# A decoder layer on one core: in the last feed-forward half, one weight group in four gets its low parts from an adding transfer

## The chip, the cores and the metric

The kernel runs on one core of one Trainium2 chip. The metric is the time of one execution on the device in microseconds (us); lower is better. A core has five engines that run side by side and wait for one another by semaphores: TensorE (PE, with its weight loads as PEld), VectorE (DVE), ScalarE (ACT), GpSimd (POOL) and SyncE (SP), which here only issues transfers. Transfers are moved by 16 DMA engines that SP's queue (q1) and POOL's queue (q0) share.

## What is computed

One layer of a decoder on 256 tokens of width 2048, in float32: a SwiGLU half-step, a mixer with three branches (gated linear attention, spatial gating, attention into a memory), a second SwiGLU half-step, and a final norm. The change is in the second half-step:

```python
D_MODEL = 2048; SEQ = 256; D_FF = 5632

def swiglu(h, w_gate, w_up, w_down):
    return (jax.nn.silu(h @ w_gate) * (h @ w_up)) @ w_down

def reference(x, ...):
    x = x + 0.5 * swiglu(rmsnorm(x, ffn1_norm[l]), ffn1_w_gate[l], ffn1_w_up[l], ffn1_w_down[l])
    h = rmsnorm(x, mix_norm[l])
    mem_n = rmsnorm(mem, mem_norm[l])
    x = x + mixer(h, mem_n, ...)
    x = x + 0.5 * swiglu(rmsnorm(x, ffn2_norm[l]), ffn2_w_gate[l], ffn2_w_up[l], ffn2_w_down[l])
    return rmsnorm(x, final_norm)
```

## The kernel before

Every large product is made three times in a shorter float format. A float32 number is split into a high part, its value cast to that format (`fp32r` in the rows), and a low part, the number less its high part. `products` (L122) issues, for a weight tile of 128 rows by 512 columns and a block of 128 tokens, high times high (L123), high times low weight (L124) and low times high weight (L125), all into one accumulator in PSUM.

`gemm` (L127) goes over a column block of 512 weight columns in groups of four weight tiles (512 rows, 1 MB). For each group `load` (L106) issues one transfer on SP's queue into a `raw` buffer, of which there are three. Each group is then taken in two halves of two tiles: ACT casts the half to `wh` (L119), VectorE subtracts to make `wl` (L120), and TensorE makes 12 matmuls with it. `wh` and `wl` have three buffers each, so ACT can be at most three halves ahead of TensorE.

The second half-step is the call of `ffn` (L309) with `final=True`. It works in two parts of 6 and 5 column blocks. A block is a `gemm` with the gate weights (16 weight tiles, so groups at 0, 4, 8 and 12), the Silu on ACT (L319), a `gemm` with the up weights, the product on VectorE (L323), and the transposition and splitting of the result (L166 on TensorE, L174 on ACT, L175 on VectorE), which TensorE reaches during the first group of the next `gemm`. After each part come four `gemm` calls with the down weights.

Larger or longer-lived tiles take one of 17 slots (`slot`, named `m8` or `m_` with a number in the rows). In the second half-step the input, the residual, the final gain and the hidden tiles of a part hold 13 of them.

The text of the kernel doesn't set the order on an engine by itself: a scheduler orders the instructions of each engine when the program is built, with costs of its own. Each engine then runs its list strictly in that order.

Of the kernel before, what the change touches and what calls it, by code (L numbers as in the profile page):

```python
# [8 lines left out]
F32 = mybir.dt.float32  # L9
# [8 lines left out]
P = 128  # L18
# [5 lines left out]
CW = 512  # L24
# [35 lines left out]
def layer(ctx: ExitStack, tc: tile.TileContext, a: dict, out: bass.AP):  # L60
# [10 lines left out]
    def slot(shape, dtype=F32):  # L71
        return big.tile(shape, dtype, name="m8", tag="m8")
# [33 lines left out]
    def load(w, row, col, parts=1):  # L106

        raw = wp.tile([P, 4, CW], F32, name="raw", tag="raw")
        n = 4 // parts
        for i in range(0, 4, n):  # L110
            r = row + i * P
            nc.sync.dma_start(
                raw[:, i : i + n, :],
                w[r : r + n * P, col : col + CW].rearrange("(j p) n -> p j n", p=P),
            )
        return raw

    def split(raw, wh, wl):
        nc.scalar.copy(wh, raw)  # L119
        nc.vector.tensor_tensor(wl, raw, wh.bitcast(F32), op=ALU.subtract)  # L120
# [3 lines left out]
        nc.tensor.matmul(acc, lhsT=lhs.h(kt, b), rhs=wl, start=False, stop=False)  # L124
        nc.tensor.matmul(acc, lhsT=lhs.l(kt, b), rhs=wh, start=False, stop=last)  # L125

    def gemm(lhs, n_tiles, w, row0, col0, accs, ticks=0, raws=(), tail=0):  # L127


        raws = list(raws)  # L130
        held = []
        for g0 in range(0, n_tiles, 4):
            raw = raws.pop(0) if raws else load(w, row0 + g0 * P, col0)
            late = g0 >= n_tiles - 4 * tail
            if late:
                both = [slot([P, 4, CW], F32R) for _ in range(2)]
                held.append((g0, *both))
            for h0 in (0, 2):
                if late:
                    wh, wl = (t[:, h0 : h0 + 2, :] for t in both)  # L140
                else:
                    wh = wp.tile([P, 2, CW], F32R, name="wh", tag="wh")
                    wl = wp.tile([P, 2, CW], F32R, name="wl", tag="wl")
                split(raw[:, h0 : h0 + 2, :], wh, wl)
                if late:
                    continue
                for b in range(NB):
                    for j in range(2):
                        kt = g0 + h0 + j
                        products(  # L150
                            lhs, kt, b, wh[:, j, :], wl[:, j, :], accs[b],
                            kt == 0, kt == n_tiles - 1,
                        )
                tick(ticks)
        for b in range(NB):
            for g0, wh, wl in held:
                for j in range(4):
                    kt = g0 + j
                    products(
                        lhs, kt, b, wh[:, j, :], wl[:, j, :], accs[b], kt == 0, kt == n_tiles - 1  # L160
                    )
# [147 lines left out]
    def ffn(xT, rs, wg, wu, wd, after, begin=lambda: None, final=False):  # L309
        done = 0  # L310
        for part, n_ch in enumerate((6, 5)):
            hT = Split(slot, 4 * n_ch)
            for c in range(n_ch):
                col = (done + c) * CW
                pg = [acc() for _ in range(NB)]
                gemm(xT, KT, wg, 0, col, pg, ticks=1)
                sil = [tmp() for _ in range(NB)]
                for b in range(NB):
                    nc.scalar.activation(sil[b], pg[b], AF.Silu, scale=rs[:, b : b + 1])  # L319
                pu = [acc() for _ in range(NB)]  # L320
                gemm(xT, KT, wu, 0, col, pu, ticks=1)
                for b in range(NB):
                    nc.vector.scalar_tensor_tensor(  # L323
                        out=sil[b], in0=pu[b], scalar=rs[:, b : b + 1], in1=sil[b],
                        op0=ALU.mult, op1=ALU.mult,
                    )
                    tsplit(sil[b], hT, 4 * c, b)
# [493 lines left out]
```

## Time and profile before

| | |
|---|---|
| median of 2 runs | 2392.0 us (2391.84 to 2392.16) |
| the profiled execution | 2390.98 us, of which the span from the first to the last instruction is 2389.3 us |
| TensorE busy | 2371.3 us, 99% of the span |
| VectorE busy | 1269.8 us, 53% |
| ScalarE busy | 1071.5 us, 45% |
| GpSimd busy | 59.6 us, 2% |
| SP's DMA queue | 442.56 MB, 56.9% of the 16 engines' time |
| gate and up blocks of the second half-step, part one | about 1636 to 1900 us of the span |

Busy shares are means over the whole span. Which engine sets the end is read from who waits for whom, and TensorE's clock from the granted clock of a stretch (1.00 is 2.4 GHz, 0.50 is 1.2 GHz).

### The profile page before, as it was taken

The page shows a single profiled execution, that of the slowest core. Times are in us where ns is not written, and L with a number is a line of the kernel's source. Part 1 is how long each engine was busy: PE and PEld are TensorE (multiplying, and loading weights), DVE is VectorE, ACT ScalarE, POOL GpSimd, SP SyncE. Part 2 cuts the span into 40 slices and gives each one's busy share as a digit, 9 for nine tenths or more (in the row PEclk, how much of TensorE's full clock was granted, in tenths as well). Part 3 has the DMA queues.
Part 4 walks back from the last instruction along what each step waited for, and adds up shares of the span by engine and source line. Part 5 has one row for each costly group of instructions (what it writes and reads, how often), then busy time and mean ns, then how long its engine had stood idle before and what let it go on. Part 6 is the DMA issues. An engine that isn't in the chain of part 4 may idle for free.

```text
span 2389.3 us, 26431 instructions
## 1 busy us (share of the span) xinstructions
PE 2371.3 (99%) x10746; PEld 1961.4 (82%) x10746; DVE 1269.8 (53%) x1330; ACT 1071.5 (45%) x1265; POOL 59.6 (2%) x57
## 2 busy tenths in 40 slices
PE   8999999999999999999999999999999999999998
PEld 6888888888888888888788888888888888888886
DVE  5644545445445556556765555555454454454454
ACT  7544444344444444435444444445444433444443
POOL 0000000000000001001200000000000000000000
PEclk9999999999999999999999999999999999999999
DMA  7565565565566665444546556655555555555564
GB/s 263 185 191 188 186 193 194 194 193 188 184 193 196 196 207 194 147 167 159 177 159 212 194 194 194 204 184 191 186 188 192 194 189 193 192 184 193 194 191 144
DMA packets 224211, 451.76 MB, mean 189 GB/s; under 512 B 7268, under 2 KB 7336, under 8 KB 223448
## 3 DMA queue, kind: packets, MB, share of 16 engines
q1 hardware_dynamic: 222344, 442.56, 56.9%
q0 software_dynamic: 1744, 7.51, 0.9%
q8 instruction: 84, 1.38, 0.2%
q14 instruction: 39, 0.32, 0.0%
HBM read 445.84 MB, written 4.19 MB: 188 GB/s over the span
## 4 chain that ended last, share of the span: by engine, by line
PE 97%; DVE 1%; issue 1%; ACT 1%; DMA 0%; ACTq 0%; POOLq 0%; POOL 0%; SPq 0%; DVEq 0%
PE acc L124 31%; PE acc L123 31%; PE acc L125 31%; PE trp L166 2%; PE sml L641 0%; DVE wl L120 0%; PE sml L546 0%; PE sml L574 0%; PE sml L449 0%; DMA m<-in_mem_dram 0%; ACT m L658 0%; ACT tmp L180 0%; ACT wh L119 0%; PE sml L695 0%; PE sml L508 0%
## 5 line engine op out<-in xcount | busy, mean ns | idle before, releaser
L120 DVE TENSOR_TENSOR wl<-raw,wh 128x1024 fp32r<-128x1024 f32 x828 | 1029.2, 1244 | 1024.5 <-ACT wh L119 1023.9
L119 ACT CAST wh<-raw 128x1024 fp32r<-128x1024 f32 x828 | 871.4, 1053 | 1161.3 <-PE acc L125 1144.5
L124 PE MATMUL acc<-wl,m 128*128 128x512 f32 x3312 | 1294.4, 391 | 1.8 <-DVE wl L120 1.8
L125 PE MATMUL acc<-wh,m 128*128 128x512 f32 x3312 | 1290.4, 390 | 0.1
L123 PE MATMUL acc<-wh,m 128*128 128x512 f32 x3312 | 1183.7, 392 | 1.8 <-ACT wh L119 0.9
L124 PEld LDWEIGHTS acc<-wl,m 128*128 128x128 f32 x3312 | 622.5, 188 | 132.2 <-DVE wl L120 3.3
L123 PEld LDWEIGHTS acc<-wh,m 128*128 128x128 f32 x3312 | 622.0, 188 | 131.3 <-ACT m L190 2.2
L125 PEld LDWEIGHTS acc<-wh,m 128*128 128x128 f32 x3312 | 622.1, 188 | 127.5 <-DVE m L191 0.5
L190 ACT ACTIVATE m<-trp,gT 128x128 fp32r<-128x128 f32 x128 | 43.0, 364 | 23.7 <-PE trp L166 14.3
L174 ACT CAST m<-trp 128x512 fp32r<-128x512 f32 x64 | 34.9, 588 | 40.9 <-PE trp L166 40.9
L175 DVE TENSOR_TENSOR m<-trp,m 128x512 fp32r<-128x512 f32 x64 | 41.7, 686 | 21.2 <-ACT m L174 20.9
L191 DVE SCALAR_TENSOR_TENSOR m<-trp,gT,m 128x128 fp32r<-128x128 f32 x128 | 41.3, 347 | 13.5 <-ACT m L190 12.3
L166 PEld LDWEIGHTS trp<-ident,tmp 128*128 128x128 f32 x288 | 34.7, 140 | 6.6
L166 PE MATMUL trp<-ident,tmp 128*128 128x128 f32 x288 | 40.0, 272 | 0.0
L319 ACT ACTIVATE tmp<-acc,rs 128x512 f32<-128x512 f32 x44 | 30.1, 690 | 19.5 <-PE acc L125 19.5
L180 ACT ACTIVATE tmp<-m 128x512 f32<-128x512 f32 x40 | 24.8, 623 | 15.6 <-DVE m L338 11.9
L323 DVE SCALAR_TENSOR_TENSOR tmp<-acc,rs,tmp 128x512 f32<-128x512 f32 x44 | 30.9, 743 | 0.0
L338 DVE SCALAR_TENSOR_TENSOR m<-acc,m 128x512 f32<-128x512 f32 x32 | 20.9, 683 | 9.8 <-PE acc L125 9.5
L203 POOL TENSOR_TENSOR rs<-rs,mhalf 128x1 f32<-128x1 f32 x8 | 4.4, 554 | 868.7 <-DVE rs L200 868.7
L166 PE MATMUL trp<-ident,m 128*128 128x128 f32 x160 | 22.8, 280 | 2.9 <-DMA m<-in_mem_dram 2.9
L166 PEld LDWEIGHTS trp<-ident,m 128*128 128x128 f32 x160 | 19.7, 144 | 6.6 <-DMA m<-in_mem_dram 3.0
L661 POOL TENSOR_TENSOR m<-m,m 128x1024 f32<-128x1024 f32 x7 | 20.9, 2992 | 115.3 <-ACT m L658 87.8
(136 smaller groups left out, 389.0 us busy)
## 6 DMA issues: line engine op xcount, KB each, us to landing
raw<-in_w_in_dram SPq DMA_DIRECT2D x96, 1024.0 KB, 5.1
raw<-in_ffn_w_gate_dram SPq DMA_DIRECT2D x88, 1024.0 KB, 5.2
raw<-in_ffn_w_up_dram SPq DMA_DIRECT2D x88, 1024.0 KB, 5.2
raw<-in_ffn_w_down_dram SPq DMA_DIRECT2D x88, 1024.0 KB, 5.1
raw<-in_w_branch_dram SPq DMA_DIRECT2D x24, 1024.0 KB, 5.1
raw<-in_w_out_dram SPq DMA_DIRECT2D x16, 1024.0 KB, 5.1
raw<-in_w_kv_mem_dram SPq DMA_DIRECT2D x14, 1024.0 KB, 5.1
m<-in_mem_dram SPq DMA_DIRECT2D x4, 512.0 KB, 8.3
```

The costliest lines, as they stand in the source:

```text
L119: nc.scalar.copy(wh, raw)
L120: nc.vector.tensor_tensor(wl, raw, wh.bitcast(F32), op=ALU.subtract)
L123: nc.tensor.matmul(acc, lhsT=lhs.h(kt, b), rhs=wh, start=first, stop=False)
L124: nc.tensor.matmul(acc, lhsT=lhs.h(kt, b), rhs=wl, start=False, stop=False)
L125: nc.tensor.matmul(acc, lhsT=lhs.l(kt, b), rhs=wh, start=False, stop=last)
L166: nc.tensor.transpose(out=ps[:, j * P : (j + 1) * P], in_=src[:, j * P : (j + 1) * P], identity=ident)
L174: nc.scalar.copy(hi, ps)
L175: nc.vector.tensor_tensor(lo, ps, hi.bitcast(F32), op=ALU.subtract)
L190: nc.scalar.activation(dst.h(kt, b), pj, AF.Copy, scale=g)
L191: nc.vector.scalar_tensor_tensor(out=dst.l(kt, b), in0=pj, scalar=g, in1=dst.h(kt, b).bitcast(F32), op0=ALU.mult, op1=ALU.subtract,)
L319: nc.scalar.activation(sil[b], pg[b], AF.Silu, scale=rs[:, b : b + 1])
L323: nc.vector.scalar_tensor_tensor(out=sil[b], in0=pu[b], scalar=rs[:, b : b + 1], in1=sil[b], op0=ALU.mult, op1=ALU.mult,)
```

## The change

In the gate and up products of the second half-step, the group at row 12 x 128 of each column block (the last of four) is no longer split by VectorE. A new function loads the group on SP's queue as before, lets ACT cast it to the high part `wh`, lets ACT also write the negated high part into `wl`, and issues on POOL's queue a second transfer of the same megabyte of weights that adds to `wl` in place. Both tiles are of four weight tiles and take slots of the 17 instead of the three-deep `wh` and `wl` buffers. The function is called at the head of `gemm`, so its load is issued ahead of the loads of groups 0, 4 and 8. There are 22 such groups, two for each of the 11 column blocks.

```diff
+    def split_by_dma(w, row, col):
+        raw = load(w, row, col)
+        wh, wl = (slot([P, 4, CW], F32R) for _ in range(2))
+        for h0 in (0, 2):
+            hs = slice(h0, h0 + 2)
+            nc.scalar.copy(wh[:, hs, :], raw[:, hs, :])
+            nc.scalar.activation(wl[:, hs, :], wh[:, hs, :].bitcast(F32), AF.Copy, scale=-1.0)
+        nc.gpsimd.dma_start(
+            wl,
+            w[row : row + 4 * P, col : col + CW].rearrange("(j p) n -> p j n", p=P),
+            accum_op=ALU.add,
+        )
+        return wh, wl
+
-    def gemm(lhs, n_tiles, w, row0, col0, accs, ticks=0, raws=(), tail=0):
+    def gemm(lhs, n_tiles, w, row0, col0, accs, ticks=0, raws=(), tail=0, added=None):
...
+        if added is not None:
+            sums = split_by_dma(w, row0 + added * P, col0)
         for g0 in range(0, n_tiles, 4):
-            raw = raws.pop(0) if raws else load(w, row0 + g0 * P, col0)
+            if g0 == added:
+                raw = None
+            else:
+                raw = raws.pop(0) if raws else load(w, row0 + g0 * P, col0)
...
             for h0 in (0, 2):
-                if late:
+                if g0 == added:
+                    wh, wl = (t[:, h0 : h0 + 2, :] for t in sums)
+                elif late:
                     wh, wl = (t[:, h0 : h0 + 2, :] for t in both)
...
-                split(raw[:, h0 : h0 + 2, :], wh, wl)
+                if raw is not None:
+                    split(raw[:, h0 : h0 + 2, :], wh, wl)
...
-                gemm(xT, KT, wg, 0, col, pg, ticks=1)
+                gemm(xT, KT, wg, 0, col, pg, ticks=1, added=12 if final else None)
...
-                gemm(xT, KT, wu, 0, col, pu, ticks=1)
+                gemm(xT, KT, wu, 0, col, pu, ticks=1, added=12 if final else None)
```

The scheduler places the new instructions. In the changed kernel's text the lines after the new function are 24 further down (L319 becomes L343, L166 becomes L190, L174 becomes L198), the new casts are L134, the negating copies L135 and the adding transfers L136.

ACT's list in the second column block of part one, gate product: before, from the cast of the second half of group 4 on. The two L174 rows split the transposed result of the block ahead, `wh_11987` and `wh_12003` are group 8, `wh_12021` and `wh_12037` group 12, and `wh_12061` opens the up product.

```order
L119 CAST wh_11969<-raw_11951 128x1024
L174 CAST m8_11613<-trp_11900 128x4x128
L174 CAST m8_11613<-trp_11908 128x4x128
L119 CAST wh_11987<-raw_11985 128x1024
L119 CAST wh_12003<-raw_11985 128x1024
L119 CAST wh_12021<-raw_12019 128x1024
L119 CAST wh_12037<-raw_12019 128x1024
L119 CAST wh_12061<-raw_12059 128x1024
```

The same place on ACT in the changed kernel. `m8_11917` is the high part of group 12, `m8_11918` its negated copy that the adding transfer completes; `m8_12058` and `m8_12059` are the pair of the up product.

```order
L119 CAST wh_11976<-raw_11958 128x1024
L198 CAST m8_11613<-trp_11898 128x4x128
L134 CAST m8_11917<-raw_11915 128x1024 x2
L198 CAST m8_11613<-trp_11906 128x4x128
L135 ACTIVATE m8_11918<-m8_11917 128x1024
L119 CAST wh_11994<-raw_11992 128x1024
L135 ACTIVATE m8_11918<-m8_11917 128x1024
L119 CAST wh_12010<-raw_11992 128x1024
L134 CAST m8_12058<-raw_12056 128x1024 x2
L119 CAST wh_12067<-raw_12065 128x1024
L135 ACTIVATE m8_12059<-m8_12058 128x1024 x2
```

The casts and copies for this group 12 stand between group 4 and group 8 of the same product, the ones for the up product's group 12 already before its group 0 is done.

TensorE's list at the end of that gate product, before: `wh_12037` and `wl_12038` are the second half of group 12, and `acc_12057`, `acc_12058` the accumulators of the up product.

```order
L124 MATMUL acc_11916<-wl_12038,m8_10912 128x512
L125 MATMUL acc_11916<-wh_12037,m8_10914 128x512
L123 MATMUL acc_11916<-wh_12037,m8_10912 128x512
L124 MATMUL acc_11916<-wl_12038,m8_10912 128x512
L125 MATMUL acc_11916<-wh_12037,m8_10914 128x512
L123 MATMUL acc_12057<-wh_12061,m8_10911 128x512
L123 MATMUL acc_12058<-wh_12061,m8_10911 128x512
L124 MATMUL acc_12057<-wl_12062,m8_10911 128x512
```

The same engine in the changed kernel where group 8 ends and group 12 begins. The first row that reads `m8_11918` waits for POOL's transfer.

```order
L125 MATMUL acc_11914<-wh_12010,m8_10914 128x512
L123 MATMUL acc_11913<-m8_11917,m8_10912 128x512
L123 MATMUL acc_11914<-m8_11917,m8_10912 128x512
L123 MATMUL acc_12054<-wh_12067,m8_10911 128x512
L123 MATMUL acc_12055<-wh_12067,m8_10911 128x512
L124 MATMUL acc_11913<-m8_11918,m8_10912 128x512
L125 MATMUL acc_11913<-m8_11917,m8_10914 128x512
L123 MATMUL acc_11913<-m8_11917,m8_10912 128x512
L124 MATMUL acc_11913<-m8_11918,m8_10912 128x512
```

Two matmuls of the up product have moved ahead of the first use of the sum; everything behind that row waits with it.

POOL's list around the start of the second half-step, before and then in the changed kernel (`rs_3` is the scale of the norm that the first Silu needs):

```order
L756 DMA m8_10915<-kept_984 128x2048
L756 DMA m8_10916<-kept_984 128x2048
L284 DMA m8_11611<-in_final_norm_dram 128x2048
L203 TENSOR_TENSOR rs_3_10910<-rs_11601,mhalf_84 128x1
L203 TENSOR_TENSOR rs_3_10910<-rs_11606,mhalf_84 128x1
L203 TENSOR_TENSOR rs_4_11610<-rs_16427,mhalf_84 128x1
```

```order
L308 DMA m8_11611<-in_final_norm_dram 128x2048
L136 DMA m8_11624<-in_ffn2_w_gate_dram 128x4x512
L227 TENSOR_TENSOR rs_3_10910<-rs_11601,mhalf_84 128x1
L227 TENSOR_TENSOR rs_3_10910<-rs_11606,mhalf_84 128x1
L136 DMA m8_11765<-in_ffn2_w_up_dram 128x4x512
L136 DMA m8_11918<-in_ffn2_w_gate_dram 128x4x512
```

The first adding transfer stands ahead of the two small operations for `rs_3`; the other 21 follow one after the other with nothing between them.

## Rows read from the trace of the kernel before

**Rows 1.** The page's part 1: busy us, share of the span, instructions.

```profile
span 2389.3 us, 26431 instructions
PE 2371.3 (99%) x10746; PEld 1961.4 (82%) x10746; DVE 1269.8 (53%) x1330; ACT 1071.5 (45%) x1265; POOL 59.6 (2%) x57
```

**Rows 2.** The page's part 4: the chain that ended last, by engine.

```profile
PE 97%; DVE 1%; issue 1%; ACT 1%; DMA 0%; ACTq 0%; POOLq 0%; POOL 0%; SPq 0%; DVEq 0%
```

**Rows 3.** Waits, whole span: who waited for whom, us in total, times, longest.

```profile
ACT wh L119 <- PE acc L125: 1144.5, 706, 3.8
DVE wl L120 <- ACT wh L119: 1023.9, 771, 3.6
...
PE acc L124 <- DVE wl L120: 1.8, 3, 0.9
```

**Rows 4.** Busy time by window: length, engines, granted clock, DMA share, GB/s.

```profile
1656.00:2016.00 360.00, 360.00 (x1618) 298.78 (x1617) 179.84 (x167) 154.72 (x163) 0.00 (x0) 1.00 0.59 190
...
2370.00:2375.00 5.00, 5.00 (x23) 4.14 (x23) 0.00 (x0) 0.00 (x0) 0.00 (x0) 1.00 0.00 0
```

**Rows 5.** Timeline: a block's transposes and the next block's, and ACT behind them.

```profile
1700.55 1.03 PE L166 MATMUL trp<-ident,tmp 128*128 128x128 f32 x8
...
1744.97 1.03 PE L166 MATMUL trp<-ident,tmp 128*128 128x128 f32 x8
1745.61 1.07 ACT L174 CAST m<-trp 128x512 fp32r<-128x512 f32 x2 [1.43 <-PE trp L166]
1746.74 1.05 ACT L119 CAST wh<-raw 128x1024 fp32r<-128x1024 f32 x1
1749.46 1.05 ACT L119 CAST wh<-raw 128x1024 fp32r<-128x1024 f32 x1 [1.67 <-PE acc L125]
1750.55 1.23 DVE L120 TENSOR_TENSOR wl<-raw,wh 128x1024 fp32r<-128x1024 f32 x1 [1.50 <-ACT wh L119]
```

**Rows 6.** Chain in order of time: the eight transposes.

```profile
1656.29 0.88 PE trp L166 x8
```

**Rows 7.** Timeline of TensorE in the last product, when VectorE and the DMA are idle.

```profile
2372.09 0.39 PE L123 MATMUL acc<-m,m 128*128 128x512 f32 x1
2372.31 0.39 PE L124 MATMUL acc<-m,m 128*128 128x512 f32 x1
2372.54 0.39 PE L125 MATMUL acc<-m,m 128*128 128x512 f32 x1
```

**Rows 8.** DMA in 1679 to 1768 us: queue, packets, MB, share; issues, us to landing.

```profile
q1 hardware_dynamic: 8448, 16.78, 58.3%
...
raw<-in_ffn_w_gate_dram SPq DMA_DIRECT2D x8, 1024.0 KB, 5.2
```

**Rows 9.** The page's part 6: transfers issued by POOL, KB each, us to landing.

```profile
m<-kept POOLq DMA_DIRECT2D x2, 1024.0 KB, 6.3
...
m<-in_final_norm_dram POOLq DMA_DIRECT2D x1, 1024.0 KB, 7.7
...
ws<-in_sg_w_s_dram POOLq DMA_DIRECT2D x1, 256.0 KB, 4.4
```

**Rows 10.** Busy time by window after TensorE's last matmul (columns as Rows 4).

```profile
2382.00:2384.00 2.00, 0.00 (x0) 0.00 (x0) 1.30 (x5) 0.47 (x1) 0.55 (x1) 1.00 0.14 51
2384.00:2386.00 2.00, 0.00 (x0) 0.00 (x0) 0.42 (x2) 0.87 (x2) 0.00 (x0) 0.64 0.57 214
2386.00:2389.00 3.00, 0.00 (x0) 0.00 (x0) 0.00 (x0) 0.00 (x0) 0.00 (x0) 0.50 0.55 207
```

## The prediction

> **What bounds the kernel now.** I read the page's shares first, then the chain that ended last, then the waits, and then the stretch that the change touches. TensorE is busy 2371.3 of 2389.3 us [rows 1] and holds 97% of the chain [rows 2]. Busy alone can mislead, since matmuls overlap, so the waits have to confirm it: ACT waits 1144.5 us for TensorE to free a `wh` buffer, VectorE waits 1023.9 us for ACT, and TensorE waits for VectorE 1.8 us in the whole run [rows 3]. So ACT is held back by the engine that it feeds, VectorE by ACT, and TensorE by nobody.
>
> In 360 us of gate and up blocks of the second half-step TensorE has no idle time at full clock, VectorE is busy 179.84 us, ACT 154.72 us, the DMA engines 59% [rows 4]. From one block's transposes to the next are 44.42 us [rows 5]. A block is 192 matmuls of 512 columns (16 weight tiles, 2 token blocks, 3 products, 2 weights) and eight transposes, and these take 0.88 us [rows 6], which leaves 43.54/192 = 0.227 us for a matmul. In the last product, where VectorE and the DMA are idle [rows 4], matmuls follow each other by 0.22 to 0.23 us as well [rows 7]. So VectorE's work doesn't slow a matmul, and there is nothing in this stretch that a lighter VectorE could give back.
>
> **What the change removes.** 22 groups of two subtractions each, 44 x 1.23 us = 54 us of VectorE [rows 5]. All of it lies beside TensorE's matmuls, so it is worth nothing on the path; the most that a lighter VectorE could give is TensorE's wait for it, 1.8 us over the whole run, nearly all outside this stretch. I take 0.
>
> **What it adds on ACT.** 44 casts become 44 others of the same kind. 44 negating copies are new. No such copy is in the trace; the nearest row is the cast of the same 128x1024 at 1.05 us [rows 5], so 46 us more on ACT in about 488 us (11 x 44.42), where it is busy 43%. What hides it is ACT's lead of up to three halves. The lead is shortest where the scheduler has put two casts and a copy between group 4 and group 8 of the same product. There, counted from the start of the transposes, ACT begins its list at 0.64 us (1745.61 less 1744.97) and runs 0.53 + 2 x 1.05 + 0.53 + 1.05 = 4.2 us before the cast for group 8, which ends at 5.9; VectorE's low part follows at about 7.2. TensorE has 31 matmuls and the transposes ahead of group 8, 7.9 us, and two more matmuls ahead of its first low part. So about 1 us of cover is left and the cost is 0; with that cover gone it would be up to 1 us at each such place. At the border from the mixer three such operations, about 3 us, stand ahead of the casts for the last group of the output product, whose lead is some 5 us less their own 2.4 us of cast and subtraction: 0 to 2 us, I take 1.
>
> **What it moves on the queues.** SP still issues four 1 MB loads a product. Group 12's comes first and holds one of three `raw` buffers until ACT's two casts, so the others go through two for a while. A load lands in 5.2 us [rows 8]; going through the lists row by row with the durations above, loads of up to 8 us leave TensorE's matmuls back to back after the border, so I take 0. POOL's 22 adding transfers have nothing queued behind them but each other, and the `rs_3` operations behind the first are needed 30 us later.
>
> **What it adds on the path: the wait for the sum.** TensorE can't do the first low-part matmul of group 12 until the adding transfer has landed, and it issues in order, so a late sum stops it for as long as it is late. How early the transfer goes out depends on where ACT's two copies stand in its list. For 17 of the 22 groups they stand so far ahead that, counted in matmuls of 0.227 us, 21 to 34 us remain. For five they don't: the gate products of the second, fourth and sixth block of part one and of the second and fourth of part two. There ACT's second copy ends at 0.64 + 2 x 0.53 + 5 x 1.05 = 6.95 us after the transposes' start, and POOL issues at about 7.0. TensorE reaches the first low-part matmul after 59 matmuls and eight transposes, 59 x 0.227 + 0.88 = 14.3 us. The margin is **7.2 us**.
>
> The trace has no adding transfer, so its landing time L is bounded by the nearest rows. From below: a plain 1 MB transfer issued by POOL, 6.3 us, another 7.7 [rows 9]; that ends inside the margin or 0.5 us outside it. From above: q1's 8448 packets took 58.3% of 16 engines over 89 us [rows 8], 98 ns a packet; a 1 MB load is 528 packets, 33 an engine, 3.2 us. An add has to read its destination too. If a packet then costs twice as much, L is 6.3 + 3.2 = 9.5 us; with one of SP's loads sharing the engines, up to 3.2 us more, 12.7. If a packet costs four times as much, 6.3 + 9.7 = 16, and with two loads beside it about 22. I take 11, the middle of the twofold case, since the engines are 58% taken and the nearest rows are plain transfers of this size. Five waits of 11 - 7.2 = 3.8 us are **19 us**.
>
> A rule speaks to this price. The Trainium skill, Collectives: The Full Stack, section "The bandwidth ceiling: the fold count and why AG ≠ RS ≠ AR", says that the add in a DMA engine costs no cycles itself and that the two source reads are what halves the rate, with a measured ratio of 1.93. No run here shows an adding transfer yet; by that ratio alone, with no load beside it, L would be 6.3 + 3.0 = 9.3 us and the sum 5 x 2.1 = 10.5 us in place of 19, a total of 2403 us.
>
> **Sum.** Against the profiled execution of 2390.98 us: -0 for VectorE, +1 at the border, +19 for the five waits: 2411. That execution is 1.0 us below the median of the runs, so the forecast is **2412 us**, 0.8% slower. A measurement of this kernel can hardly tell less than 2% (48 us) from no change.
>
> **Rivals.**
>
> *The sum is always in time (0.2).* If an add is as quick as a plain transfer, L is 6.3 to about 7.5 us, and at most 0.3 us is missing in five places: 2391 to 2395 us, not slower by anything that counts. For it: the 6.3 us row and the margin of 7.2. Against it: the destination must be read as well, and the other 1 MB transfer took 7.7 us.
>
> *Adding is several times slower than copying (0.2).* From L = 7.2 + 48/5 = 16.8 us on, the five waits alone are worth 2%. At 22 us they cost 5 x 14.8 = 74 us, and the first group of the half-step, with 21 us of margin, begins to wait too: about 2466 us. From about 30 us on most groups wait, and then the 22 transfers are the pace: each wait grows one for one. Beside it goes the share of the DMA engines: a product of 21.8 us has 4 x 3.2 = 13 us of loads, so an adding transfer that takes the engines more than 9 us makes them the bound.
>
> *TensorE's clock.* After the last matmul, at 2380.4 us, the granted clock is still 1.00 in 2382 to 2384 us, 0.64 in the next 2 us, then 0.50, the lower of its two levels [rows 10]. The waits that I forecast are as short as the idle time ahead of the first of these rows, where it is still full, so I add nothing. A longer one may end at 1.2 GHz; if the next 12 matmuls of 0.227 us then took twice as long, each of the five would cost 2.7 us more, 14 in all: 2426 us or, with the longer wait itself, some 2432. It is in the upper half of the forecast's own case.
>
> *A gain (0.03).* Only if something freed by VectorE speeds TensorE, against [rows 4, 7]: 2385 to 2390 us.
>
> *The change doesn't do what it says.* It does: the lists show 44 subtractions fewer and 22 adding transfers.
>
> **How the numbers follow.** Forecast (L of 7.5 to 16 us, five waits of 0.3 to 9 us, with or without the clock): 2393 to 2440 us, chance 0.57. In time: 0.2. Slow adding: 0.2. Gain: 0.03. The range leaves out the gain and the upper half of slow adding: 2390 to 2465 us. Faster by over 2% takes a gain that no row offers: 0.01. Slower by over 2% is the slow adding and the edge of the forecast with the clock: 0.22. Within 2%: 0.77.
>
> **What the changed kernel's profile would show.** TensorE's waits should list the low-part matmul of group 12 waiting for the adding transfer, five times, about 4 us each, and no other new wait of over 2 us; the blocks of part one should alternate, 44.4 us and then some 48. POOL's issues should show the adding transfer landing after 9 to 13 us, and the DMA share of the stretch should rise from 0.59 to about 0.75 if a packet counts twice. VectorE should fall by 54 us and ACT rise by 46 without any trace of it in the time. I am wrong if the landing time is outside 7.5 to 16 us, or if ACT's longer list delays a `wh` cast that TensorE waits for.

## The result, and the profile after

The changed kernel takes **2423.3 us** (two runs, 2421.23 and 2425.35), 1.0131 times the kernel before, 95% interval 1.0087 to 1.0174: 1.3% slower. The forecast was 2412 us, its range 2390 to 2465. The profiled execution is the one of 2425.35 us, with a span of 2423.6 us, 34.3 us more than before.

The page's part 1 of the changed kernel, to be held against [rows 1]:

```profile
PE 2386.4 (98%) x10746; PEld 1967.0 (81%) x10746; DVE 1216.2 (50%) x1286; ACT 1104.9 (46%) x1309; POOL 87.9 (4%) x79
```

VectorE has lost 53.6 us of work and ACT has gained 33.4. TensorE does the same 10746 instructions and is busy 15.1 us longer; the other 19.2 us of the longer span are idle time. So the time went in two ways, and each needs a view of its own. First the waits of the changed kernel (us in total, times, longest):

```profile
PE acc L124 <- DMA m<-in_ffn_w_gate_dram: 15.1, 5, 5.5
PE acc L124 <- DVE wl L120: 4.1, 8, 0.9
...
PE acc L123 <- ACT wh L119: 2.6, 5, 1.0
```

The first row is new: the low-part matmul of a gate product's group 12 waits for the adding transfer, in five places. They are the five that the prediction named: in 1640 to 2340 us these waits end at 1721.85, 1815.99, 1910.33, 2135.28 and 2229.75 us. Against [rows 3], where TensorE waited 1.8 us for VectorE, little else is new, and none of it is longer than 1.0 us.

The first of the five on the timeline of POOL and, in a second view, of TensorE (start us, us, instruction, idle before and what ended it):

```profile
1708.82 1.28 POOL L136 DMA_DIRECT2D m<-in_ffn_w_gate_dram  x1 [41.03 <-issue]
1716.33 1.27 POOL L136 DMA_DIRECT2D m<-in_ffn_w_up_dram  x1 [6.23 <-ACT m L135]
```

```profile
1715.69 0.61 PE L123 MATMUL acc<-wh,m 128*128 128x512 f32 x2
1721.85 0.80 PE L124 MATMUL acc<-m,m 128*128 128x512 f32 x1 [5.54 <-DMA m<-in_ffn_w_gate_dram]
1722.44 0.63 PE L125 MATMUL acc<-m,m 128*128 128x512 f32 x1
1722.87 0.63 PE L123 MATMUL acc<-m,m 128*128 128x512 f32 x1
1723.29 0.63 PE L124 MATMUL acc<-m,m 128*128 128x512 f32 x1
```

POOL issues at 1708.82 us, TensorE is ready for the sum at about 1716.2 (two matmuls of 0.227 us from 1715.69), and gets it at 1721.85: a margin of 7.4 us, and 13.0 us until the sum is there. In the other four places the margin is 7.5 us and the sum is there after 9.7 to 10.4 us. Behind the wait the matmuls follow each other by 0.43 us and not by 0.23 as in [rows 7]. That is the second way in which time went, and the windows of the same kernel show it (columns as in [rows 4]; the last but two is the granted clock). The first four rows belong to this wait, the next three to the one that ends at 1910.33, the last two to the one that ends at 2229.75:

```profile
1718.00:1720.00 2.00, 0.00 (x0) 0.00 (x0) 0.22 (x1) 0.00 (x0) 0.00 (x0) 0.93 1.05 391
1720.00:1722.00 2.00, 0.15 (x1) 0.16 (x1) 0.00 (x0) 0.00 (x0) 0.00 (x0) 0.50 1.08 329
1722.00:1724.00 2.00, 2.00 (x5) 1.61 (x6) 0.02 (x1) 1.05 (x1) 0.00 (x0) 0.50 1.10 262
...
1726.00:1728.00 2.00, 2.00 (x9) 1.64 (x8) 0.00 (x0) 0.01 (x1) 0.00 (x0) 0.86 1.10 262
```

```profile
1908.00:1910.00 2.00, 0.03 (x1) 0.00 (x0) 1.02 (x1) 0.00 (x0) 0.74 (x1) 1.00 1.05 347
1910.00:1912.00 2.00, 1.67 (x5) 1.36 (x6) 0.00 (x0) 0.26 (x1) 0.00 (x0) 0.72 1.06 400
1912.00:1914.00 2.00, 2.00 (x6) 1.52 (x6) 1.18 (x1) 0.79 (x1) 0.00 (x0) 0.50 1.08 259
...
2228.00:2230.00 2.00, 0.25 (x1) 0.25 (x2) 0.12 (x1) 0.00 (x0) 0.00 (x0) 1.00 1.04 368
2230.00:2232.00 2.00, 2.00 (x10) 1.60 (x10) 0.00 (x0) 0.68 (x1) 0.00 (x0) 1.00 1.07 325
```

The granted clock falls from 2.4 to 1.2 GHz, five or six matmuls fit in 2 us in place of nine or ten, and it is back 4 to 6 us after the wait. Behind the waits of 5.54 and 2.76 us the fall begins while TensorE still stands (0.93 in 1718 to 1720 us above), behind those of 2.30 and 2.40 us only after it has resumed. The wait of 2.08 us leaves the clock full, and once, at 2270 us, it falls behind two short waits of 0.99 and 0.52 us for a cast and its subtraction. Over the 17 windows of 2 us between 1640 and 2340 us in which it is below 0.97, TensorE's busy time times what is missing of the clock sums to 10.4 us; 8.8 of them lie behind the four late sums, the rest at 2270 us.

The block that holds the first late sum, from the transposes at its head to those at the head of the next, and that next one, on TensorE's timeline of the changed kernel:

```profile
1701.83 0.60 PE L190 MATMUL trp<-ident,tmp 128*128 128x128 f32 x4
...
1754.78 0.60 PE L190 MATMUL trp<-ident,tmp 128*128 128x128 f32 x4
...
1798.79 0.60 PE L190 MATMUL trp<-ident,tmp 128*128 128x128 f32 x4
```

52.95 us and 44.01, where [rows 5] have 44.42. The five blocks with a late sum take 52.95, 50.82, 48.63, 49.20 and 47.84 us: 27.3 of the 34.3 us lie in them.

The transfers on the DMA side, by the page's part 3 (packets, MB, share of 16 engines) and by the issues over the whole span (KB each, median us to landing):

```profile
q1 hardware_dynamic: 222344, 442.56, 54.5%
q0 software_dynamic: 13360, 30.58, 6.2%
```

```profile
m<-in_ffn_w_gate_dram POOLq DMA_DIRECT2D x11, 1024.0 KB, 10.2
m<-in_ffn_w_up_dram POOLq DMA_DIRECT2D x11, 1024.0 KB, 12.9
```

POOL's queue had 0.9% of the engines before. 6.2% x 16 x 2423.6 less 0.9% x 16 x 2389.3 is 2060 us of one engine for 22 transfers, 5.9 us of all 16 for each, against 3.2 for one of SP's loads [rows 8]: 1.8 times as much. The loads feel it. Of those issued in 1690 to 1900 us, 18 of the up weights take a median of 8.4 us to land where they took 5.2.

### The profile page after: what moved, and what is told of

Same layout as the page of the kernel before. It is cut to its first block, busy times and chain, and to the rows that moved or that the text cites. A ratio compares the mean times of both kernels' runs of the same rounds, so it can differ in the third digit from the quotient of the medians.

```text
span 2423.6 us, 26439 instructions
## 1 busy us (share of the span) xinstructions
PE 2386.4 (98%) x10746; PEld 1967.0 (81%) x10746; DVE 1216.2 (50%) x1286; ACT 1104.9 (46%) x1309; POOL 87.9 (4%) x79
## 4 chain that ended last, share of the span: by engine, by line
PE 84%; issue 8%; DMA 4%; ACT 2%; DVE 1%; POOL 0%; ACTq 0%; POOLq 0%; SPq 0%; DVEq 0%
PE acc L124 27%; PE acc L125 27%; PE acc L123 27%; DMA raw<-in_ffn_w_up_dram 2%; PE trp L190 2%; DMA m<-in_ffn_w_gate_dram 1%; DVE wl L120 1%; ACT wh L119 1%; DMA raw<-in_ffn_w_gate_dram 1%; PE sml L665 0%; ACT m L134 0%; PE sml L570 0%; PE sml L598 0%; ACT m L135 0%; PE sml L473 0%
## 5 line engine op out<-in xcount | busy, mean ns | idle before, releaser
L120 DVE TENSOR_TENSOR wl<-raw,wh 128x1024 fp32r<-128x1024 f32 x784 | 974.2, 1244 | 1080.2 <-ACT wh L119 1079.8
L119 ACT CAST wh<-raw 128x1024 fp32r<-128x1024 f32 x784 | 823.6, 1052 | 1098.9 <-PE acc L125 1042.8
L124 PE MATMUL acc<-wl,m 128*128 128x512 f32 x3136 | 1228.2, 392 | 4.1 <-DVE wl L120 4.1
L125 PE MATMUL acc<-wh,m 128*128 128x512 f32 x3136 | 1223.5, 391 | 0.1
L123 PE MATMUL acc<-wh,m 128*128 128x512 f32 x3136 | 1128.2, 392 | 3.5 <-ACT wh L119 2.6
L124 PEld LDWEIGHTS acc<-wl,m 128*128 128x128 f32 x3136 | 589.8, 188 | 130.0 <-DVE wl L120 8.0
L123 PEld LDWEIGHTS acc<-wh,m 128*128 128x128 f32 x3136 | 589.2, 188 | 128.1 <-ACT wh L119 5.5
L125 PEld LDWEIGHTS acc<-wh,m 128*128 128x128 f32 x3136 | 589.5, 188 | 120.2 <-DVE m L215 0.5
L124 PE MATMUL acc<-m,m 128*128 128x512 f32 x192 | 79.0, 411 | 15.1 <-DMA m<-in_ffn_w_gate_dram 15.1
L125 PE MATMUL acc<-m,m 128*128 128x512 f32 x192 | 78.3, 408 | 0.0
L123 PE MATMUL acc<-m,m 128*128 128x512 f32 x192 | 76.4, 402 | 0.0
L134 ACT CAST m<-raw 128x1024 fp32r<-128x1024 f32 x44 | 44.1, 1049 | 45.9 <-DMA raw<-in_ffn_w_up_dram 38.5
L124 PEld LDWEIGHTS acc<-m,m 128*128 128x128 f32 x192 | 38.4, 200 | 25.4 <-DMA m<-in_ffn_w_gate_dram 17.2
L343 ACT ACTIVATE tmp<-acc,rs 128x512 f32<-128x512 f32 x44 | 30.1, 689 | 45.2 <-PE acc L125 45.2
L198 ACT CAST m<-trp 128x512 fp32r<-128x512 f32 x64 | 35.5, 586 | 29.5 <-PE trp L190 29.5
L135 ACT ACTIVATE m<-m 128x1024 fp32r<-128x1024 f32 x44 | 45.0, 1054 | 0.0
L125 PEld LDWEIGHTS acc<-m,m 128*128 128x128 f32 x192 | 38.2, 199 | 8.2
L123 PEld LDWEIGHTS acc<-m,m 128*128 128x128 f32 x192 | 37.6, 196 | 8.2
```

Of the source, the lines that this page charges most:

```text
L123: nc.tensor.matmul(acc, lhsT=lhs.h(kt, b), rhs=wh, start=first, stop=False)
L134: nc.scalar.copy(wh[:, hs, :], raw[:, hs, :])
L135: nc.scalar.activation(wl[:, hs, :], wh[:, hs, :].bitcast(F32), AF.Copy, scale=-1.0)
L198: nc.scalar.copy(hi, ps)
```

## The experiments

Their times stand against the kernel before on the same chip: 2391.3 to 2391.7 us, medians of 21 to 29 runs. Three explanations were held against each other. **Theory A**: five sums come late, and the clock falls behind them. **Theory B**: the adding transfers hold back SP's loads, so ACT's casts come late. **Rival C**: ACT's longer list, with the early load and cast for group 12, holds back the casts by itself. A fourth, **T**, came later: the traffic has a price wherever it lies.

**No adding transfer.** The transfer is left out, so the negated high part serves as low part.

```diff
-        nc.gpsimd.dma_start(
-            wl,
-            w[row : row + 4 * P, col : col + CW].rearrange("(j p) n -> p j n", p=P),
-            accum_op=ALU.add,
-        )
```

> The changed kernel without its 22 adding transfers: the low parts of group 12 are left as the negated high parts, so the sums of those groups are left out. ACT's list is that of the changed kernel, and the first low-part matmul of group 12 waits for ACT's copies alone, which end 7.5 us or more ahead of it. Theory A (the five late sums, and the lower clock behind them, are the loss): no low-part wait on a transfer, the clock 1.00 in the whole stretch, 2391 to 2396 us. Rival B (the added traffic delays SP's loads, and ACT with them): also 2391 to 2396 us, so this run doesn't part A from B. Rival C (ACT's 44 extra copies and the early load of group 12 delay the casts): the waits of TensorE for ACT and VectorE in the stretch, 4 us, stay, and the time is 2396 to 2405 us.

Measured: 2391.94 us, ratio 1.0002 (0.9993 to 1.0011). ACT's 44 more operations, the early load and the slots cost nothing here, and VectorE's 44 subtractions less bring nothing. Rival C falls for the changed kernel's own order.

**A plain copy.** The line with `accum_op` alone is taken out: the same megabytes on the same queue at the same places, but the low part is the weight itself.

> The same 22 transfers issued by POOL at the same places, but copying over the low part in place of adding to it, so the addition is left out. It prices the add itself. Margin of the five short places by the list: 8.1 us. Theory A: a plain transfer of 1 MB landed after 6.3 to 7.8 us, so the waits vanish or are under 1 us each: 2392 to 2397 us. Rival B (a second reader on the DMA engines is what hurts, added or not): landing 9 us or more, waits of 1 to 3 us in five places, 2400 to 2412 us.

Measured: 2392.7 us, ratio 1.0006 (0.9998 to 1.0015). The page's queue row and the waits:

```profile
q0 software_dynamic: 13360, 30.58, 4.1%
```

```profile
PE acc L124 <- DMA m<-in_ffn_w_gate_dram: 1.7, 2, 0.9
```

By the same working as above a copy is 3.5 us of all engines, an add 5.9. The copies of the gate weights land after a median of 6.1 us. In the five short places they take 5.5 to 8.5 us, so three are in time and two just late. So the cost hangs on the adding.

**Every sum one product earlier.** The groups are loaded, cast, copied and added during the product ahead of their own, from its head on. `ahead()` calls `split_by_dma` for the next product.

```diff
+        ahead()
         for g0 in range(0, n_tiles, 4):
...
+                gemm(
+                    xT, KT, wg, 0, col, pg, ticks=1, added=late, sums=coming,
+                    ahead=lambda: make("up", wu, col),
+                )
```

> All 22 sums as in the changed kernel, but each made one product ahead: the load, the copies and the adding transfer for the next product's group 12 stand in the program before the loop of the present product. The smallest margin by the list is 23.8 us, where the adding transfers landed after 10 to 13 us. Theory A: the five waits of 15 us in all and the lower clock behind them go, 2392 to 2399 us. Rival B (traffic): the DMA share stays at 0.75, the waits of TensorE for ACT and VectorE stay at 4 us with the clock's falls behind them, 2400 to 2410 us. Rival C (ACT's list): the same as B, with the waits at other places.

Measured: 2425.67 us, ratio 1.0144 (1.0130 to 1.0158). No matmul waits for a sum any more, and nothing is won. The waits:

```profile
PE acc L123 <- ACT wh L119: 18.6, 10, 4.1
PE acc L124 <- DVE wl L120: 4.9, 9, 0.9
```

Theory A seemed refuted. The timeline of ACT and, in a second view, of TensorE in this kernel tells what happened instead:

```profile
1726.76 1.05 ACT L119 CAST wh<-raw 128x1024 fp32r<-128x1024 f32 x1 [1.36 <-PE acc L125]
1733.77 1.99 ACT L134 CAST m<-raw 128x1024 fp32r<-128x1024 f32 x2 [5.95 <-DMA raw<-in_ffn_w_up_dram]
1735.66 1.04 ACT L119 CAST wh<-raw 128x1024 fp32r<-128x1024 f32 x1
```

```profile
1736.76 0.73 PE L123 MATMUL acc<-wh,m 128*128 128x512 f32 x2 [1.87 <-ACT wh L119]
```

ACT stands 5.95 us for the load of a group that TensorE doesn't need in this product. The `wh` cast that TensorE needs next is behind it in ACT's list. So the experiment took one wait away and made another: it isn't a test of theory A alone. Whether the transfers (B) or the list (C) make that wait, the later kernels tell.

**Spare matmuls against the clock.** In the gate product of the five blocks with a late sum, 16 matmuls into an accumulator that nobody reads are added: 80 x 0.227 = 18.2 us of filler.

```diff
+            if g0 == added and fill:
+                spare = sml()
+                for _ in range(fill):
+                    nc.tensor.matmul(
+                        spare, lhsT=lhs.h(0, 0), rhs=sums[0][:, 0, :], start=True, stop=True
+                    )
```

> The changed kernel with 16 spare matmuls (0.227 us each, 3.6 us) ahead of group 12 in the gate product of every second block, into a bank that nobody reads. They stand where TensorE sat idle, in the five places with a short margin, which becomes 11.1 us. If the idle time is what lowers the clock (theory A), 5 x 3.6 = 18 us of spare matmuls take the place of some 12 us of waits, 0 to 2 us of wait are left in each place, and the matmuls at half clock behind them (about 10 us of loss) go: 2412 to 2418 us, and the clock at 1.00 behind these places. If the clock falls for another reason, such as the traffic, the spare matmuls come on top of it: 2426 to 2432 us.

Measured: 2428.35 us, ratio 1.0154 (1.0141 to 1.0168). The waits for the sum are gone (18.2 us in five places, 3.6 us each, is enough), and in none of the windows of 2 us does the clock fall. The time misses the first forecast and lies in the range of the second, but not by its way, since the clock stayed full. There are 7.1 us of waits for `wh` and 7.0 for `wl`, and they come as in the kernel above: before 1731.88 us ACT stands 5.69 us for the load of the next group 12. In the changed kernel the cast at this place begins at 1732.83 us without any wait: TensorE's own halt of 5.5 us had given the load that time. One wait had covered the other. Less its 18.2 us of filler this kernel still takes 2410 us, 19 more than the kernel before, without a late sum and at full clock: with the sums in time, waits behind late loads take their place. How much the clock costs this run can't say, as the waits moved.

**Adding transfers in half of the products.** First in the up products alone (`added` is dropped from the gate call), then in the gate products alone (dropped from the up call).

> Adding transfers in the up products alone: 11 in place of 22, one every 44.4 us, each with about 23 us ahead of its use; the gate products are those of the kernel before. Theory A: no sum is late, 2391 to 2394 us. Theory B: never two adding transfers together, so no load is late either: 2391 to 2394 us. Theory T: half of what the 22 cost, so 2405 to 2410 us.

Measured: 2391.62 us, ratio 1.0000 (0.9991 to 1.0009), no wait of 0.2 us or more and no fall of the clock in 1640 to 2340 us. T falls: eleven adding transfers with about 23 us of time each are free. They land after a median of 10.6 us, the one issued at 1712.32 us after 13.4.

> Adding transfers in the gate products alone: 11, five of them with a margin of about 9 us, and issues 62, 20 and 69 us apart, so never two together. Theory A: five waits of landing time less 9 us; landing 10 to 13 us gives 1 to 4 us each, 5 to 20 us in all, and half the clock behind those over 2 us, up to 10 more: 2396 to 2415 us, with the waits on the low-part matmul for the transfer. Theory B: an adding transfer without another near it lands in 9 to 10 us and delays no load by much: 2391 to 2396 us, TensorE's waits for wh under 2 us in all. Theory T: half of what the 22 cost, 2405 to 2410 us, in waits for wh.

Measured: 2396.88 us, ratio 1.0023 (1.0015 to 1.0032). The waits, and the last of the five places in the windows:

```profile
PE acc L124 <- DMA m<-in_ffn_w_gate_dram: 3.7, 5, 1.3
...
PE acc L124 <- DVE wl L120: 1.7, 3, 0.9
PE acc L123 <- ACT wh L119: 0.9, 2, 0.6
```

```profile
2208.00:2210.00 2.00, 1.01 (x4) 0.86 (x5) 1.23 (x1) 0.28 (x1) 0.00 (x0) 1.00 1.05 407
2210.00:2212.00 2.00, 2.00 (x10) 1.65 (x9) 0.00 (x0) 0.00 (x0) 0.00 (x0) 1.00 1.05 381
```

A margin of about 9 us and five waits of 0.7 us in the mean, so a lone adding transfer lands in some 10 us; the median is 10.1. The waits are all for the sum, none for loads, and behind waits of up to 1.3 us the clock stays at 1.00. The 5.2 us stand at theory A's low end: no wait was long enough for its part on the clock.

**The third group in place of the fourth.** `added=8` in both calls; TensorE comes to the sum 6 us sooner.

> The group whose low part is made by the adding transfer is the third of its product (rows at 8 x 128) in place of the fourth: the same 22 transfers are issued at nearly the same places, but TensorE comes to the sum some 6 us sooner. Counted on the lists, five sums have about 1 us, three 16 to 18 us, the rest more. Theory A: each of the five waits grows by about 6 us, from 3 to about 9 to 12 us, 45 to 60 us in all, and with half the clock behind them some 10 us more: 2445 to 2465 us. Theory B: the transfers and the loads are as bunched as in the changed kernel; TensorE stands still anyway and the loads catch up meanwhile, so the time goes with the longest lateness at each bunch: the waits for wh fall while those for the sum grow, 2435 to 2455 us. Theory T: 2420 to 2428 us as in the changed kernel.

Measured: 2447.43 us, ratio 1.0232 (1.0218 to 1.0246). The waits:

```profile
PE acc L124 <- DMA m<-in_ffn_w_gate_dram: 26.6, 5, 6.1
PE acc L123 <- ACT wh L119: 14.6, 7, 3.2
```

The total lies in the ranges of both A and B, and neither is right inside: the waits for `wh` grew, where B had them fall, and the five waits for the sum grew to 5.3 us only, where A had 9 to 12, because TensorE is halted some 2.7 us just ahead of each, for a `wh` cast. No load makes that one; in 1703 to 1713 us ACT is busy without a gap, with the casts and copies of two such groups. The cover of about 1 us that the prediction found for ACT's list is there in the changed kernel, and gone when the whole is asked for one group sooner.

**The same 22 transfers, earlier but at other places of the product ahead.** `ahead()` is called behind the third group (at `g0 == 12`) and, later, behind the first (at `g0 == 4`).

```diff
         for g0 in range(0, n_tiles, 4):
+            if g0 == 12:
+                ahead()
```

> All 22 adding transfers stay, but each group's load, casts and negating copies are asked for in the middle of the product ahead of its own. Counted on the lists, every sum has at least 24 us, and the adding transfers go out 14 to 31 us apart, instead of four in 48 us and then none for 47 us. Theory A (late sums): nothing is late, 2391 to 2394 us. Theory B (bunched adding transfers hold up SP's loads, so ACT's casts come late): an adding transfer is about 5.9 us of all 16 engines and a load 3.2; 14 us then hold 2.6 loads and one add, 8.2 + 5.9 = 14.1 us of engine time, so the engines are full only at the nearest pairs; 2392 to 2404 us, with TensorE's waits for wh under half of the 18.6 us of the kernel whose sums were made one product ahead. Theory T (the total of traffic counts, wherever it lies): 2420 to 2428 us, as with sums one product ahead.

Measured: 2405.12 us, ratio 1.0059 (1.0047 to 1.0072), 1 us outside what B allowed, with 5.1 us of waits for `wh`. Spreading helps, but the first block of part one is 4.1 us longer than before, the stretch with the down products and part two's first block 5.7, the nine other blocks some 5 us together. That left open whether the distance between transfers or their place in the lists counts.

> All 22 adding transfers, each group asked for in the product ahead of its own but after that product's first group: every sum has at least 24 us, and the issues stand about 8, 19, 23 and 39 us apart, between the bunch of 6, 15, 13 and 54 us that gave 2426 us and the even spread of 14 to 31 us that gave 2405. Theory B: the time lies between these two, 2408 to 2420 us, with the waits for wh at the pairs that stand 8 us apart. If only the distance of the nearest pair counts, 2420 to 2428 us; if a sum that has time enough is all that counts beside the border of each part, 2403 to 2408 us.

Measured: 2397.24 us, ratio 1.0025 (1.0016 to 1.0034), below all that was expected. POOL's issues and, in a second view, ACT, at the place shown above for the kernel with the sums at the head:

```profile
1708.68 1.27 POOL L136 DMA_DIRECT2D m<-in_ffn_w_up_dram  x1 [31.06 <-ACT m L135]
1717.24 1.28 POOL L136 DMA_DIRECT2D m<-in_ffn_w_gate_dram  x1 [7.28 <-ACT m L135]
1738.76 1.27 POOL L136 DMA_DIRECT2D m<-in_ffn_w_up_dram  x1 [20.25 <-ACT m L135]
```

```profile
1723.69 1.05 ACT L119 CAST wh<-raw 128x1024 fp32r<-128x1024 f32 x1 [1.29 <-PE acc L125]
1726.41 1.05 ACT L119 CAST wh<-raw 128x1024 fp32r<-128x1024 f32 x1 [1.67 <-PE acc L125]
1729.13 1.05 ACT L119 CAST wh<-raw 128x1024 fp32r<-128x1024 f32 x1 [1.67 <-PE acc L125]
1733.38 2.00 ACT L134 CAST m<-raw 128x1024 fp32r<-128x1024 f32 x2 [3.19 <-DMA raw<-in_ffn_w_up_dram]
...
1736.24 1.03 ACT L119 CAST wh<-raw 128x1024 fp32r<-128x1024 f32 x1
```

The pair 8.6 us apart is still there, and the next 21 us behind it: nearly the issue times of the kernel that took 2425.67 us. ACT waits for the early group here too, 3.19 us in place of 5.95. But three `wh` casts stand between the Silu and that wait, where the other list has one (1726.76 us), and with that lead TensorE doesn't notice. From the second block of each part on, a block is 44.43 to 44.47 us again; of the 5.3 us by which this trace's span is longer than before, 3.6 lie in the two first blocks and the border between the parts. ACT's wait for the early groups over the whole run, here and in the kernel with `ahead()` behind the third group, whose transfers are evenly spread (columns: busy, mean ns | idle before, and what ended most of it):

```profile
L134 ACT CAST m<-raw 128x1024 fp32r<-128x1024 f32 x44 | 44.0, 1048 | 26.5 <-DMA raw<-in_ffn_w_up_dram 17.1
```

```profile
L134 ACT CAST m<-raw 128x1024 fp32r<-128x1024 f32 x44 | 44.3, 1047 | 62.4 <-DMA raw<-in_ffn_w_gate_dram 33.8
```

With the sums at the head of the product ahead it waits 51.0 us (the row stands below). So the loads are less late here, and that is part of the difference. But the evenly spread kernel has ACT waiting longest and loses 13.5 us where the one with 51.0 loses 34. So neither the distance between the transfers, my reading until then, nor the lateness of the loads sets the price by itself; by the lists it matters whether an urgent cast stands behind a late load. (The lists differ in more places than this one, so it is a reading of the traces, not shown by an edit of this one cast.)

**Taking the transfers out of the early kernel.** The kernel with the sums at the head of the product ahead, without the transfer and then with a plain copy (the two edits of above).

> The kernel whose 22 groups are loaded, cast and copied one product ahead, without the adding transfers: TensorE takes the negated high part as low part. The lists of ACT and TensorE stay nearly as they were. Theory B (the adding transfers take the engines' time from SP's loads): with them gone the waits for wh go too, 2391 to 2394 us. Rival C (ACT runs its list in order, and the casts for a group asked for so early stand in the way of the casts that TensorE needs next, whatever the transfers do): the 18.6 us of waits for wh and the fallen clock stay, 2415 to 2426 us.

> The same kernel with plain copies of the same megabytes in place of adding transfers, so the low part is the weight itself. By the queues' shares a copy takes some 3.5 us of all 16 engines and an add 5.9. Theory B: three transfers in about 28 us with loads of 3.2 us, four to a product of 21.8 us, ask for 3 x 5.9 + 16.4 = 34 us of the engines when they add and 3 x 3.5 + 16.4 = 27 us when they copy, so the loads keep up: waits for wh under 5 us in all, 2392 to 2398 us. Rival C, and any cost of a transfer on POOL's queue as such: as with adding, 2415 to 2426 us.

Measured: 2392.12 us, ratio 1.0003 (0.9994 to 1.0012), without it; 2394.03 us, 1.0009 (1.0001 to 1.0018), with copies. ACT's wait for the early loads, by the groups of the two and, last, of the kernel with adding transfers (busy, mean ns | idle before, and what ended it):

```profile
L134 ACT CAST m<-raw 128x1024 fp32r<-128x1024 f32 x44 | 44.0, 1049 | 19.4 <-DMA raw<-in_ffn_w_gate_dram 11.1 <-PE acc L124 4.2 <-DMA raw<-in_ffn_w_up_dram 4.2
```

```profile
L134 ACT CAST m<-raw 128x1024 fp32r<-128x1024 f32 x44 | 44.0, 1049 | 30.3 <-DMA raw<-in_ffn_w_gate_dram 20.6 <-DMA raw<-in_ffn_w_up_dram 9.7
```

```profile
L134 ACT CAST m<-raw 128x1024 fp32r<-128x1024 f32 x44 | 43.9, 1047 | 51.0 <-DMA raw<-in_ffn_w_up_dram 25.6 <-DMA raw<-in_ffn_w_gate_dram 25.4
```

ACT's idle time for these loads is 15, 30 and 51 us as a transfer takes 0, 3.5 and 5.9 us of the engines (of the first row's 19.4 us, 4.2 are for TensorE). The list alone is harmless; the transfers slow the loads, and by the traces above the list decides whether TensorE has to wait for it. B and C are halves of one mechanism.

**First blocks without.** The evenly spread kernel with VectorE's subtraction kept in the first column block of each part, 18 adding transfers.

```diff
-                late = 12 if final else None
+                late = 12 if final and c else None
...
-                    if final:
+                    if final and (c or key == "gate"):
```

> The evenly spread kernel, but the first column block of each of the two parts keeps the subtraction on VectorE: 18 adding transfers. In the kernel with 22 the first blocks were 4.1 and 5.7 us longer than before, the nine others 5 us in all. Theory B with the border of a part as its tightest place: these first blocks go back to 44.4 us, and what is left is about 5 us, 2395 to 2398 us. Theory T, a price per transfer: 18/22 of the 13.5 us, 2402 to 2403 us.

Measured: 2398.1 us, ratio 1.0030 (1.0019 to 1.0041). Just above B's 2398, and under T's 2402. One first block goes back to 44.42 us; the other part's border is 175.9 us and not 180.7, but its second block now takes 47.64 us. About half of the evenly spread kernel's loss was at the borders, and part of it moved one block on.

No version is faster than the kernel before. Of those that still add, the one with adding transfers in the up products alone equals it.

## Why the prediction was right, and where its sum was short

**VectorE, worth 0: right.** 53.6 us fewer, and the kernels without adding transfers, and the one that adds in the up products alone, stay within 0.1% of before. **ACT, worth 0 and up to 1 us at the border: right** for the changed kernel; a group sooner the cover is gone (2.7 us in five places). It rose by 33.4 us, not 46: the 44 copies are busy 45.0 us, but operations that overlap are counted once.

**The five late sums: right in place and mechanism, a little high.** Margin 7.2 us foreseen, 7.4 to 7.5 read. Landing 11 taken; in the five places it is 13.0, 10.4, 10.0, 10.1 and 9.7 us. Five waits of 3.8 us, 19 in all; measured 5.54, 2.76, 2.30, 2.40 and 2.08, together 15.1. Why the first landed late isn't shown. It isn't the next adding transfer, which POOL issues 7.5 us behind it: in the other four places one follows 6.4 to 7.1 us behind, and these land as soon as lone ones, 10.1 us in the median of the kernel with gate products only. A lone one can be as late: 13.4 us, once, in the kernel with up products only. It is the second of such a pair that is slow, 13.3 to 14.2 us, and it has time. Reading the destination was priced at twice a packet; it came to 1.8 times a load, and the share of the DMA engines in 1656 to 1856 us went from 0.59 to 0.75, as foreseen. The ratio that the prediction quotes from the Trainium skill (Collectives: The Full Stack, "The bandwidth ceiling: the fold count and why AG ≠ RS ≠ AR"), 1.93, gave an estimate of 9.3 us for the landing: near the 10.1 us of a lone add, short of the 13.0 us of the first late sum.

**The clock, put at 0: the step that failed.** The prediction argued that its waits are as short as the idle time ahead of the first of [rows 10], where the clock is still full. By its own numbers they aren't: the last matmul ends at 2380.4 us, so the idle time is 1.6 us at the start of that row and 3.6 at its end, and the waits were forecast at 3.8. And those rows say how long the record stays full, not that work which begins by then is safe. Behind a wait of 2.30 us it is 0.72 in the window in which TensorE starts again and 0.50 in the next, while TensorE is at work. The rival on TensorE's clock had the mechanism and nearly the price: 2.7 us for each of five places, 14 in all, where four places cost 1.7 to 3.1 us, 8.8 in all. That its total of 2426 us meets the 2425.35 of the profiled execution is luck: its waits were 4 us too long, its clock 5 us too dear, and the small waits and the unassigned rest that it lacked make that up. I had put it in the forecast's upper half and out of the sum. The sum foresaw 20 of the 34.3 us; the time stayed inside the range because the range was wide.

**Loads of up to 8 us leave matmuls back to back: off by a few us.** The loads of the up weights take 8.4 us in the median, and TensorE's small waits for `wh` and `wl` grew to 6.7 us, against 2.7 us before (1.8 for `wl` in [rows 3] and 0.9 for `wh`). The prediction named a late `wh` cast as a second way to be wrong, but by ACT's longer list. It isn't the list: without the transfers these waits are 3.0 us.

So of the 34.3 us, TensorE's listed idle time is 19.2, of which 15.1 are the sums, and the clock 10.4. The other 4.7 I can't assign row by row; each wait is listed from the modelled end of a matmul (0.39 us behind its start, where the next would start after 0.227), so some 0.2 us of each of the 13 waits between 1640 and 2340 us is not in the list. That is about 2 us; the rest stays open.

**What stays open.** Why the clock fell behind waits of 0.99 and 0.52 us and not behind one of 2.08 us, no run here tells apart. In the evenly spread kernel, too, it fell behind 1.42 and 0.53 us and not behind 1.90 and 0.53. That the clock's cost and the waits add up as told rests on the windows; the kernel with spare matmuls shows that the clock stays full when TensorE isn't halted for the sum, but it brought waits of its own.

## What to carry to other kernels

Work that lies wholly beside the engine that sets the end gives nothing when it is moved, and the move can add a wait: here it took 54 us from VectorE, and the kernel without the transfers was no faster for it. Before an operation is given to a transfer, read how many us lie between the issue and the use at the worst place in the engines' lists; 17 of the 22 sums had 21 us or more by the lists and came in time, five had 7 and lengthened their blocks by 27 us. On an engine that runs its list in order, look for an early, patient cast ahead of an urgent one when the loads slow down: the same 22 transfers, none of them late, cost 34 us or 6, and the traces put the difference on how late the loads were and where their casts stood.

## What was not expected of the hardware

- Waits of 2.30, 2.40 and 2.76 us on TensorE cost another 1.7, 1.7 and 3.1 us in granted clock. It fell to 0.50, behind the two shorter ones after TensorE had resumed, and was back 4 to 6 us after the wait; matmuls were 0.43 us apart in place of 0.227. A wait of 2.08 us left it at 1.00.
- POOL's own instruction for an adding transfer of 1 MB takes 1.28 us, for the plain copy of the same shape 0.74. The add takes 1.7 times the copy's time on the DMA engines (5.9 against 3.5 us of all 16).
